# Input modulation one feature block further ahead, an earlier second weight block, and idle products between the first norm's steps

## The chip, the core and the metric

The kernel runs on one core of a Trainium2 chip. The core has a matrix engine (TensorE, PE in the rows), two engines for elementwise work (VectorE, DVE, and ScalarE, ACT), GpSimd (POOL) and a queue that issues transfers (SyncE, SP). Each works through its own list of instructions in order and waits for others by semaphores. The metric is the time of one execution on the device, in microseconds.

## What is computed

One layer of a hybrid transformer over 512 latent tokens and 256 context tokens, 1024 features wide. The part that matters here is its beginning: both streams are normalized and modulated, then projected. The context goes through the same weights with its own modulation vector.

```python
mod = jax.nn.silu(c) @ w_mod[layer] + b_mod[layer]
sh1, sc1, gt1, sh2, sc2, gt2 = jnp.split(mod[:, None, :], 6, axis=-1)
...
h = modulate(rmsnorm(x, g_norm_mix[layer]), sh1, sc1)          # h * (1 + scale) + shift
hc = modulate(rmsnorm(ctx, g_norm_mix[layer]), csh1, csc1)
mix_lat, mix_ctx = token_mixer(h, hc, cos, sin, layer, w_in[layer], ...)
```

Behind it come latent attention, a gated linear recurrence in both directions, an output projection, a second norm, a SwiGLU feed-forward part and a last norm.

## The kernel before

Features lie on the partitions, in 8 blocks of 128 (KT = 8); tokens lie along the free axis. Weights come in blocks of 128x1024 float32 (`make_unit`, L119 to L134): one transfer of 512 KB into a tile `wf` on SP's queue, a cast to `wh` on ScalarE (L132), the rest `wl` by subtraction on VectorE (L133). A main product is three matmuls, L150 to L152: high by high, high by low, low by high (`mm3`).

The first stage makes the modulated input and, at the same time, the first projection (`hi`, which fills `vt`). `squares` (L307, L309) adds up the squares of the 8 blocks of x in `acl`. After 32 matmuls on a tile of ones, which give nothing that is used (`warm`, L351, bank `pw`), `rstd_sums` (L174) sums `acl` over the partitions, `rstd_cols` works out 1/sqrt, `rstd_diag` (L207, L209) writes it on diagonals `rsd`, and `rstd_spread` (L216) spreads them to all partitions with four 128x128 matmuls.

The modulation of a feature block k has three steps. `modvec(k)` multiplies the block's columns of w_mod (two 512 KB transfers, `wms` or `wm`) by silu(c) in eight 32-column matmuls (L320) and copies the result from PSUM on VectorE (L323). `modsel(k)` picks the two vectors out of it with two small matmuls (L329) and makes scale and shift `ab` in three small VectorE operations (L332 to L334). `make_h(k)` then writes the block: L339 on VectorE (scale and norm), L340 on ScalarE (shift, cast to `hh`), L341 on VectorE (the rest, `hl`).

The loop at L376 goes over the blocks. In a round k stand the main products of block k for token tile 0, then `modsel(k + 1)` and `make_h(k + 1)`, the products of tile 1, `modvec(k + 2)`, and the products of tiles 2 and 3 (`g0_mm`). A weight block serves two feature blocks, so the second one is first needed at block 2, the third one at block 4. In between lie the squares of the context (from round 1), its sums (L174, round 2) and its spread (round 3); the context's products follow four rounds later. A scheduler with priorities makes the order of each engine from this code, so that neighbouring rounds overlap in it.

SP's queue is written out by hand in the line `for step in (...)`: a number up to 16 loads the columns `wm` up to there, two per feature block; 101 to 103 load the weight blocks 1 to 3; -1 and -2 load the halves of the context `xc`. Small SBUF tiles hold `modvec`'s result: `spk` for even blocks, `modsb` for odd ones.

Of the kernel before, what the change touches and what calls it, by code (L numbers as in the profile page):

```python
# [18 lines left out]
P = 128  # L19
DM = 1024  # L20
KT = DM // P
NL = 512
# [30 lines left out]
def block_kernel(ctx: ExitStack, tc: tile.TileContext, xT, ctxT, vec, cin, cst, msk, wm, wmt, wi, wqkv, wo, wgu, wd, out):  # L53
    nc = tc.nc
# [7 lines left out]
    def nm(s):  # L62
        uid[0] += 1
        return f"{s}_{uid[0]}"
# [4 lines left out]
    def sm():  # L69
        return psum.tile([P, 512], F32, tag="sm", name=nm("sm"), bufs=4)  # L70
# [15 lines left out]
    ones = L0.tile([P, P], F32, name="ones")  # L86
# [10 lines left out]
    def C(name):  # L97
        a, b = CC[name]
        return cs[:, a:b]
# [40 lines left out]
    def prefetch(n):  # L140
        while len(made) < min(n, len(units)):
            make_unit(len(made))
# [97 lines left out]
    for p, tag, n in ((E, "eb", 3), (E, "ea", 2), (D, "da", 2), (D, "db", 2), (D, "dc", 2)):  # L240
        t = p.tile([P, n, UNIT], F32, tag=tag, name=nm("wms"), bufs=1)
        wsp += [t[:, i, :] for i in range(n)]
    B = pool("B", "right")
    hh = B.tile([P, KT, NL], F32R, name="hh")
    hl = B.tile([P, KT, NL], F32R, name="hl")
# [3 lines left out]
    xs = A.tile([P, KT, NL], F32, name="xs")  # L249
# [14 lines left out]
            nc.sync.dma_start(f, wm[u])  # L264
            wms.append(f)

    for step in (2, 101, 4, 6, -1, 102, 8, -2, 10, 12, 103, 14, 16):
        if step < 0:
            nc.sync.dma_start(xc[:, -4 * step - 4 : -4 * step, :], ctxT[:, -4 * step - 4 : -4 * step, :])
        elif step > 100:  # L270
            prefetch(step - 100)
        else:
            load_wm(step)
# [38 lines left out]
    rl, rc = acl, acc  # L312

    def modvec(k):
        ps = sm()
        for j in range(2):
            f = wms[2 * k + j]
            for kk in range(4):
                g = kk
                nc.tensor.matmul(ps[32 * g : 32 * g + 32, :256], csil[:, 4 * j + kk, :], f[:, kk * 256 : (kk + 1) * 256],  # L320
                                 start=(j == 0), stop=(j == 1), skip_group_check=True, tile_position=(0, 32 * g))
        sb = A.tile([P, 256], F32, tag="modsb", name=nm("modsb"), bufs=1) if k % 2 else spk[:, NL:]
        nc.vector.tensor_copy(sb, ps[:, :256])  # L323
        return sb

    def modsel(k, sb):
        p2 = sm()
        for j in range(2):
            nc.tensor.matmul(p2[:, 2 * j : 2 * j + 2], sb[:, j * P : (j + 1) * P], C("sel"), start=True, stop=True,  # L329
                             skip_group_check=True)  # L330
        ab = A.tile([P, 4], F32, tag="ab", name=nm("ab"), bufs=KT)
        nc.vector.tensor_scalar(ab[:, 0:2], p2[:, 0:2], bm[:, 8 + k : 9 + k], 1.0, op0=ALU.add, op1=ALU.add)  # L332
        nc.vector.tensor_scalar(ab[:, 0:2], ab[:, 0:2], V("gmix")[:, k : k + 1], None, op0=ALU.mult)
        nc.vector.tensor_scalar(ab[:, 2:4], p2[:, 2:4], bm[:, k : k + 1], None, op0=ALU.add)  # L334
        return ab

    def make_h(src, r, n, k, ab, j, oh, ol):
        t = temp(n)
        nc.vector.scalar_tensor_tensor(t, src[:, k, :], ab[:, j : j + 1], r, op0=ALU.mult, op1=ALU.mult)  # L339
        nc.scalar.activation(oh[:, k, :], t, AF.Identity, bias=ab[:, 2 + j : 3 + j])  # L340
        nc.vector.scalar_tensor_tensor(ol[:, k, :], t, ab[:, 2 + j : 3 + j], oh[:, k, :].bitcast(F32), op0=ALU.add,  # L341
                                       op1=ALU.subtract)
# [4 lines left out]
    pw = sm()  # L347

    def warm(n):
        for _ in range(n):  # L350
            nc.tensor.matmul(pw[:, :P], ones, ones, start=True, stop=True, skip_group_check=True)  # L351

    warm(32)
    cols = rstd_cols(A, rstd_sums([acl], NL), DM, fast=True)
    sb = modvec(0)
    dg = rstd_diag(A, cols)
    abs_ = [modsel(0, sb)]
    pb = rstd_spread(dg)
    make_h(xs, pb, NL, 0, abs_[0], 0, hh, hl)
    nc.scalar.copy(rl, pb)  # L360
    sb = modvec(1)
    g0 = [big(), big()]
    vacc = [g0[0][:, 0, :], g0[0][:, 1, :], g0[1][:, 0, :], g0[1][:, 1, :]]

# [11 lines left out]
    for k in range(max(KT, lag + KT // 2)):  # L376
        if k < KT:
            g0_mm(k, (0,))
        if k + 1 < KT:
            abs_.append(modsel(k + 1, sb))  # L380
            make_h(xs, rl, NL, k + 1, abs_[k + 1], 0, hh, hl)
        if k == 1:
            squares(xc, acc, NC)
        if k == lag - 2:
            ccols = rstd_cols(A, rstd_sums([acc], NC), DM, fast=True)
        if k == lag - 1:
            rc = rstd_spread(rstd_diag(A, ccols))
            nc.scalar.copy(acc, rc[:, :NC])
            rc = acc
        if k < KT:  # L390
            g0_mm(k, (1,))
            if k + 2 < KT:
                sb = modvec(k + 2)
            g0_mm(k, (2, 3))
        if k >= lag - 1:
            for kc in range((k + 1 - lag) * 2, min(KT, (k + 2 - lag) * 2)):
                make_h(xc, rc, NC, kc, abs_[kc], 1, gh, gl)
        if k == lag:
            vacc += [sm(), sm()]
        if k >= lag:  # L400
            for kc in range((k - lag) * 2, min(KT, (k + 1 - lag) * 2)):
                g0_mm(kc, (4, 5))
# [41 lines left out]
    for j in range(2):  # L444
        t = HG.tile([P, 4, P], F32, name=f"am{j}")
# [447 lines left out]
    for i in range(len(seq)):  # L893
# [10 lines left out]
        h, t = seq[i]  # L904
# [258 lines left out]
```

## Time and profile before

| | |
|---|---|
| median of 3 runs | 794.73 us (791.47 to 798.05) |
| the profiled execution | 792.62 us, of it span 790.8 us |
| TensorE busy | 768.1 us, 97% of the span |
| VectorE, ScalarE busy | 446.9 us (57%), 311.4 us (39%) |
| TensorE's granted clock, mean over the span | 0.988 |
| transfers | 88.77 MB, mean 112 GB/s |

The span is the time from the first to the last instruction of the profiled execution; some 1.8 us lie around it. Times in the rows are counted from the span's start. A granted clock of 1.00 is 2.4 GHz, 0.50 is 1.2 GHz. In a row of the timeline the bracket at the end tells how long the engine was idle before it and what ended that. Matmuls are pipelined, so the distance between two starts tells more than a single duration; a product of 32-bit operands counts as two instructions there.

### The profile page before, as it was taken

The page shows a single profiled execution, that of the slowest core. Times are in us where ns is not written, and L with a number is a line of the kernel's source. Part 1 is how long each engine was busy: PE and PEld are TensorE (multiplying, and loading weights), DVE is VectorE, ACT ScalarE, POOL GpSimd, SP SyncE. Part 2 cuts the span into 40 slices and gives each one's busy share as a digit, 9 for nine tenths or more (in the row PEclk, how much of TensorE's full clock was granted, in tenths as well). Part 3 has the DMA queues.
Part 4 walks back from the last instruction along what each step waited for, and adds up shares of the span by engine and source line. Part 5 has one row for each costly group of instructions (what it writes and reads, how often), then busy time and mean ns, then how long its engine had stood idle before and what let it go on. Part 6 is the DMA issues. An engine that isn't in the chain of part 4 may idle for free.

```text
span 790.8 us, 10832 instructions
## 1 busy us (share of the span) xinstructions
PE 768.1 (97%) x4342; PEld 631.7 (80%) x4342; DVE 446.9 (57%) x820; ACT 311.4 (39%) x569; POOL 10.1 (1%) x18
## 2 busy tenths in 40 slices
PE   8899999999999989999999999999999999999995
PEld 7568878788887768888999888888888888888885
DVE  5576569839778989985566434432333233223324
ACT  6344246434544577664344223222322222212211
POOL 0000000000000100000000000000000000000000
PEclk8899999999999999999999999999999999999997
DMA  9923723311110022345403343423232323332303
GB/s 332 390 76 134 252 80 108 133 57 55 64 55 28 28 80 90 125 165 181 160 2 100 113 160 133 151 89 107 80 107 82 104 78 96 93 100 80 111 3 107
DMA packets 26706, 88.77 MB, mean 112 GB/s; under 512 B 2976, under 2 KB 5280, under 8 KB 26528
## 3 DMA queue, kind: packets, MB, share of 16 engines
q1 hardware_dynamic: 25568, 87.03, 33.0%
q10 hardware_dynamic: 1088, 1.05, 0.4%
q8 instruction: 34, 0.56, 0.3%
q14 instruction: 16, 0.13, 0.1%
HBM read 85.97 MB, written 2.10 MB: 111 GB/s over the span
## 4 chain that ended last, share of the span: by engine, by line
PE 89%; DVE 7%; ACT 2%; issue 1%; DMA 1%; SPq 0%; DVEq 0%; ACTq 0%
PE big L150 18%; PE big L151 17%; PE big L152 17%; PE sm L150 9%; PE sm L151 9%; PE sm L152 9%; PE big L857 2%; PE sm L604 1%; PE sm L876 1%; PE big L858 1%; PE sm L320 1%; DVE U L585 1%; PE sm L598 1%; DVE acl L309 1%; DVE G L506 1%
## 5 line engine op out<-in xcount | busy, mean ns | idle before, releaser
L133 DVE TENSOR_TENSOR wl<-wf,wh 128x1024 fp32r<-128x1024 f32 (+2 forms) x100 | 119.6, 1196 | 186.3 <-ACT wh L132 186.2
L132 ACT CAST wh<-wf 128x1024 fp32r<-128x1024 f32 (+2 forms) x100 | 102.9, 1029 | 280.3 <-PE big L151 167.6
L150 PE MATMUL big<-h2h,wh 128*128 128x512 f32 (+1 forms) x368 | 140.3, 381 | 0.0
L151 PE MATMUL big<-h2l,wh 128*128 128x512 f32 (+1 forms) x368 | 140.0, 381 | 0.0
L152 PE MATMUL big<-h2h,wl 128*128 128x512 f32 (+1 forms) x368 | 140.0, 381 | 0.0
L151 PEld LDWEIGHTS big<-h2l,wh 128*128 128x128 f32 x368 | 69.2, 188 | 14.6
L150 PEld LDWEIGHTS big<-h2h,wh 128*128 128x128 f32 x368 | 69.2, 188 | 14.4
L152 PEld LDWEIGHTS big<-h2h,wl 128*128 128x128 f32 x368 | 69.2, 188 | 14.4
L150 PE MATMUL sm<-ah,wh 128*128 128x512 f32 (+1 forms) x198 | 73.5, 371 | 0.0
L152 PE MATMUL sm<-ah,wl 128*128 128x512 f32 (+1 forms) x198 | 73.4, 371 | 0.0
L151 PE MATMUL sm<-al,wh 128*128 128x512 f32 (+1 forms) x198 | 73.4, 370 | 0.0
L427 DVE SCALAR_TENSOR_TENSOR wl<-wl,cs 128x1024 f32<-128x1024 f32 x32 | 39.0, 1220 | 33.8 <-DMA wl<-in_wmt_dram 33.8
L150 PE MATMUL big<-wh,hh 128*128 128x512 f32 x96 | 40.2, 422 | 3.3 <-ACT hh L340 1.9
L150 PEld LDWEIGHTS sm<-ah,wh 128*128 128x128 f32 x198 | 37.3, 188 | 7.1
L151 PEld LDWEIGHTS sm<-al,wh 128*128 128x128 f32 x198 | 37.3, 188 | 7.1
L152 PEld LDWEIGHTS sm<-ah,wl 128*128 128x128 f32 x198 | 37.3, 188 | 7.1
L150 PE MATMUL big<-hh,wh 128*128 128x512 f32 x104 | 42.8, 412 | 0.0
L151 PE MATMUL big<-hl,wh 128*128 128x512 f32 x104 | 40.9, 394 | 0.0
L152 PE MATMUL big<-hh,wl 128*128 128x512 f32 x104 | 40.8, 392 | 0.0
L151 PE MATMUL big<-wl,hh 128*128 128x512 f32 x96 | 38.8, 406 | 0.0
L152 PE MATMUL big<-wh,hl 128*128 128x512 f32 x96 | 38.4, 402 | 0.0
L506 DVE RECIPROCAL G<-S 128x528 f32<-128x528 f32 x8 | 27.5, 3432 | 0.1
(326 smaller groups left out, 1353.4 us busy)
## 6 DMA issues: line engine op xcount, KB each, us to landing
wf<-in_wgu_dram SPq DMA_DIRECT2D x44, 512.0 KB, 3.4
wl<-in_wmt_dram SPq DMA_DIRECT2D x32, 512.0 KB, 3.5
wf<-in_wi_dram SPq DMA_DIRECT2D x25, 512.0 KB, 3.9
wf<-in_wd_dram SPq DMA_DIRECT2D x16, 512.0 KB, 3.5
wms<-in_wm_dram SPq DMA_DIRECT2D x11, 512.0 KB, 9.6
wf<-in_wo_dram SPq DMA_DIRECT2D x8, 512.0 KB, 3.5
wf<-in_wd_dram SPq DMA_DIRECT2D x8, 384.0 KB, 3.1
wm<-in_wm_dram SPq DMA_DIRECT2D x5, 512.0 KB, 10.2
```

Source lines behind the costliest of these rows:

```text
L132: nc.scalar.copy(hi[:, :w], f[:, :w])
L133: nc.vector.tensor_sub(lo[:, :w], f[:, :w], hi[:, :w].bitcast(F32))
L150: nc.tensor.matmul(o, lh, rh, start=start, stop=False, skip_group_check=True)
L151: nc.tensor.matmul(o, lh, rl, start=False, stop=False, skip_group_check=True)
L152: nc.tensor.matmul(o, ll, rh, start=False, stop=stop, skip_group_check=True)
L309: nc.vector.tensor_add(acc_, acc_, sq_)
L320: nc.tensor.matmul(ps[32 * g : 32 * g + 32, :256], csil[:, 4 * j + kk, :], f[:, kk * 256 : (kk + 1) * 256], start=(j == 0), stop=(j == 1), ...
L427: nc.vector.scalar_tensor_tensor(f, f, 1.0, sc, op0=ALU.mult, op1=ALU.mult, accum_out=acc)
L506: nc.vector.reciprocal(I, S)
L585: nc.vector.scalar_tensor_tensor(U[:, c1, :], U[:, c0, :], er[:, 1, c0 : c0 + 1], U[:, c1, :], op0=ALU.mult, op1=ALU.add)
L598: nc.tensor.matmul(t, a2[:, j, :], vt[:, j, h * P : (h + 1) * P], start=True, stop=False, skip_group_check=True)
L857: nc.tensor.matmul(ps[:, 0, :], L, R[:, :NL], start=(i == 0), stop=(i == 4), skip_group_check=True)
```

## The change

Three things. The second weight block (102) is loaded as what follows the fourth pair of transfers in the list, ahead of the columns of block 2, where it stood behind those and the first half of the context. `modsel` and `make_h` run two blocks ahead of the products in a round and `modvec` three, where it was one and two; block 1 is made before the loop, with the norm read straight from PSUM (`pb`). And `warm_on` adds 3 idle products behind `modvec(0)`, on its copied result, and 8 behind `modvec(1)`, on the last diagonal; they write to `pw` and nothing reads it.

```diff
-    for step in (2, 101, 4, 6, -1, 102, 8, -2, 10, 12, 103, 14, 16):
+    for step in (2, 101, 4, 102, 6, 8, -1, 10, -2, 12, 103, 14, 16):
...
+    def warm_on(t, n):
+        for _ in range(n):
+            nc.tensor.matmul(pw[:, :P], ones, t, start=True, stop=True, skip_group_check=True)
+
     warm(32)
     cols = rstd_cols(A, rstd_sums([acl], NL), DM, fast=True)
-    sb = modvec(0)
+    sbs = [modvec(0)]
+    warm_on(sbs[0][:, :P], 3)
     dg = rstd_diag(A, cols)
-    abs_ = [modsel(0, sb)]
+    abs_ = [modsel(0, sbs[0])]
     pb = rstd_spread(dg)
     make_h(xs, pb, NL, 0, abs_[0], 0, hh, hl)
     nc.scalar.copy(rl, pb)
-    sb = modvec(1)
+    sbs.append(modvec(1))
+    warm_on(dg[0][:, 3, :], 8)
+    abs_.append(modsel(1, sbs[1]))
+    make_h(xs, pb, NL, 1, abs_[1], 0, hh, hl)
+    sbs.append(modvec(2))
...
-        if k + 1 < KT:
-            abs_.append(modsel(k + 1, sb))
-            make_h(xs, rl, NL, k + 1, abs_[k + 1], 0, hh, hl)
+        if k + 2 < KT:
+            abs_.append(modsel(k + 2, sbs[k + 2]))
+            make_h(xs, rl, NL, k + 2, abs_[k + 2], 0, hh, hl)
...
-            if k + 2 < KT:
-                sb = modvec(k + 2)
+            if k + 3 < KT:
+                sbs.append(modvec(k + 3))
```

What the scheduler makes of it is seen in the engines' lists. TensorE from `modvec(0)` to the first main products, before (`sm` are small PSUM tiles, `big` those of the main products, `wms` columns of w_mod):

```order
L320 MATMUL sm_241<-wms_77,csil 32x256 x8
L329 MATMUL sm_256<-cs,spk 128x2 x2
L216 MATMUL sm_263<-rsd_251,ones 128x128 x4
L320 MATMUL sm_273<-wms_77,csil 32x256 x4
L150 MATMUL big_284<-wh_110,hh 128x512
L150 MATMUL big_285<-wh_110,hh 128x512
L151 MATMUL big_284<-wl_111,hh 128x512
L151 MATMUL big_285<-wl_111,hh 128x512
L320 MATMUL sm_273<-wms_78,csil 32x256 x4
```

and the same place in the change (L355 are the idle products):

```order
L320 MATMUL sm_241<-wms_77,csil 32x256 x8
L355 MATMUL sm_194<-spk,ones 128x128 x3
L329 MATMUL sm_259<-cs,spk 128x2 x2
L216 MATMUL sm_266<-rsd_254,ones 128x128 x4
L355 MATMUL sm_194<-rsd_254,ones 128x128 x2
L320 MATMUL sm_276<-wms_77,csil 32x256 x4
L355 MATMUL sm_194<-rsd_254,ones 128x128 x5
L320 MATMUL sm_276<-wms_78,csil 32x256 x4
L355 MATMUL sm_194<-rsd_254,ones 128x128
L150 MATMUL big_315<-wh_110,hh 128x512
```

All of `modvec(1)` and all eleven idle products stand ahead of the first main product now; before, half of `modvec(1)` stood behind four of them.

TensorE around the sums of the context norm (L174), before; the rows that follow these up to the first product of block 4 are the selection, the spread and two `modvec` among six main products:

```order
L150 MATMUL big_284<-wh_121,hh 128x512
L151 MATMUL big_284<-wl_122,hh 128x512
L150 MATMUL big_285<-wh_121,hh 128x512
L151 MATMUL big_285<-wl_122,hh 128x512
L152 MATMUL big_284<-wh_121,hl 128x512
L174 MATMUL sm_387<-ones,acc 128x2 x2
L320 MATMUL sm_402<-wms_80,csil 32x256 x4
L320 MATMUL sm_402<-wms_81,csil 32x256 x4
```

and in the change, from the selection products of block 4 to the first product of block 4 with the third weight block (`wh_135`):

```order
L329 MATMUL sm_408<-cs,spk 128x2 x2
L152 MATMUL big_315<-wh_118,hl 128x512
L151 MATMUL big_316<-wl_119,hh 128x512
L152 MATMUL big_316<-wh_118,hl 128x512
L150 MATMUL big_316<-wh_118,hh 128x512
L151 MATMUL big_316<-wl_119,hh 128x512
L152 MATMUL big_316<-wh_118,hl 128x512
L174 MATMUL sm_418<-ones,acc 128x2 x2
L320 MATMUL sm_433<-wms_81,csil 32x256 x4
L320 MATMUL sm_433<-wm_131,csil 32x256 x4
L329 MATMUL sm_453<-cs,modsb_442 128x2 x2
L216 MATMUL sm_467<-rsd_464,ones 128x128 x2
```

The next row there is the product of block 4. The sums moved from the start of block 3's products to their end, and selection and spread follow them without a main product in between. VectorE has, in the change, between the selection of block 4 (`ab_411`) and the context norm's columns:

```order
L333 TENSOR_SCALAR ab_411<-ab_411,vc 128x2
L339 SCALAR_TENSOR_TENSOR spk<-xs,ab_411,acl 128x512
L309 TENSOR_TENSOR acc<-acc,sp_75 128x256 x2
L341 SCALAR_TENSOR_TENSOR hl<-spk,ab_411,hh 128x512
L309 TENSOR_TENSOR acc<-acc,sp_75 128x256 x2
L191 TENSOR_SCALAR rsv_421<-sm_418 128x2
```

The last of the additions to `acc`, which the sums read, now stand behind the modulation of block 4; before, they stood behind that of block 3. On ScalarE the cast of the second weight block (`wh_121` before, `wh_118` now) moved from behind the modulation of block 2 to ahead of that of block 1, and the cast of the third one from behind the first context blocks to right behind the context norm's diagonal. From the end of the loop on, the lists are the same but for a few neighbours that change places on SP and VectorE.

## Rows read from the trace of the kernel before

**Rows 1.** The page: TensorE's busy time; shares of the chain that ended last.

```profile
PE 768.1 (97%) x4342; PEld 631.7 (80%) x4342; DVE 446.9 (57%) x820; ACT 311.4 (39%) x569; POOL 10.1 (1%) x18
...
PE 89%; DVE 7%; ACT 2%; issue 1%; DMA 1%; SPq 0%; DVEq 0%; ACTq 0%
```

**Rows 2.** Stretches of time: length, engines' busy time (instructions), clock, DMA share, GB/s.

```profile
13.50:14.00 0.50, 0.50 (x15) 0.26 (x8) 0.28 (x3) 0.16 (x1) 0.00 (x0) 0.94 1.01 410
...
20.00:21.00 1.00, 1.00 (x3) 0.81 (x3) 0.68 (x2) 0.11 (x1) 0.00 (x0) 0.50 1.03 406
...
24.00:24.50 0.50, 0.50 (x5) 0.41 (x4) 0.00 (x0) 0.00 (x0) 0.00 (x0) 0.82 1.03 410
...
35.00:40.00 5.00, 3.71 (x24) 2.77 (x26) 3.39 (x10) 1.14 (x2) 0.00 (x0) 1.00 0.75 301
...
50.00:90.00 40.00, 40.00 (x200) 32.32 (x199) 27.16 (x46) 12.85 (x17) 1.94 (x6) 1.00 0.48 163
```

**Rows 3.** Timeline of TensorE: start, length, instruction, [idle before, what ended it].

```profile
12.30 1.05 PE L174 MATMUL sm<-ones,acl 128*128 128x2 f32 x8 [0.96 <-DVE acl L309]
...
15.17 1.01 PE L329 MATMUL sm<-cs,spk 128*128 128x2 f32 x4 [0.53 <-DVE spk L323]
16.04 2.06 PE L216 MATMUL sm<-rsd,ones 128*128 128x128 f32 x8
18.03 1.08 PE L320 MATMUL sm<-wms,csil 128*32 128x256 f32 x8
19.70 1.22 PE L150 MATMUL big<-wh,hh 128*128 128x512 f32 x2 [0.58 <-ACT hh L340]
...
24.54 0.71 PE L152 MATMUL big<-wh,hl 128*128 128x512 f32 x2
25.17 0.64 PE L320 MATMUL sm<-wms,csil 128*32 128x256 f32 x8
25.74 0.50 PE L150 MATMUL big<-wh,hh 128*128 128x512 f32 x1
26.08 0.40 PE L151 MATMUL big<-wl,hh 128*128 128x512 f32 x1
26.31 0.40 PE L152 MATMUL big<-wh,hl 128*128 128x512 f32 x1
...
31.79 0.50 PE L150 MATMUL big<-wh,hh 128*128 128x512 f32 x1 [1.08 <-ACT wh L132]
...
35.38 0.50 PE L329 MATMUL sm<-cs,modsb 128*128 128x2 f32 x4
...
38.20 0.50 PE L150 MATMUL big<-wh,hh 128*128 128x512 f32 x1 [1.29 <-ACT hh L340]
...
39.47 0.53 PE L174 MATMUL sm<-ones,acc 128*128 128x2 f32 x4
...
46.08 0.73 PE L150 MATMUL big<-wh,hh 128*128 128x512 f32 x2 [0.35 <-ACT wh L132]
```

**Rows 4.** Timeline of VectorE, as rows 3.

```profile
14.69 0.42 DVE L323 COPY spk<-sm 128x256 f32<-128x256 f32 x1 [0.16 <-PE sm L320]
...
18.80 1.22 DVE L133 TENSOR_TENSOR wl<-wf,wh 128x1024 fp32r<-128x1024 f32 x1
...
38.85 0.42 DVE L309 TENSOR_TENSOR acc<-acc,sp 128x256 f32<-128x256 f32 x1
```

**Rows 5.** Timeline of ScalarE, as rows 3.

```profile
26.70 0.40 ACT L307 ACTIVATE acc<-xc 128x256 f32<-128x256 f32 x1
...
30.08 0.72 ACT L340 ACTIVATE hh<-t,ab 128x512 fp32r<-128x512 f32 x1 [2.06 <-DVE t L339]
30.71 1.03 ACT L132 CAST wh<-wf 128x1024 fp32r<-128x1024 f32 x1
```

**Rows 6.** SP's issue of the second weight block; from issue to landing, us, last number.

```profile
11.74 0.33 SPq L122 DMA_DIRECT2D wf<-in_wi_dram  x1
...
wf<-in_wi_dram SPq DMA_DIRECT2D x1, 512.0 KB, 11.2
```

## The prediction

> **What bounds the kernel now.** I read the page's first part and its chain of waits, then stretches of time with clock and engine load, then the first 50 us of TensorE, VectorE and ScalarE instruction by instruction, then the transfers. TensorE is busy 97% of the span and carries 89% of the chain that ended last [rows 1]. From 50 to 90 us it is busy all of the 40 us [rows 2]. So what the edit wins or loses before 46 us arrives at the end; and from the end of the loop that the diff touches on, the order of work on every engine is the old one again, bar two or three neighbours that change places. What has to be found is one shift: when the first main product of feature block 4 (L150, 46.08 us [rows 3]) starts, and how fast TensorE runs just behind it.
>
> Up to that point TensorE loses time in two ways. It waits: 0.58 us before the first main product, 1.08 for the cast of the second weight block, 1.29 for a modulated block, 0.35 for the third weight block [rows 3]. And its clock is at the lower level (0.50, 1.2 GHz) from 13.94 us (a mean of 0.94 in the half microsecond from 13.5 is 0.44 at 1.00 and 0.06 at 0.50) to 24.18 (0.82 in that from 24.0) [rows 2]. What it did before that fall: 0.96 us idle, then 1.05 us of 128x2 products [rows 3] and some of the 32-column ones behind them. Before the rise it had run main products and 32-column ones without a pause since 19.70, 4.48 us.
>
> **The transfers.** The second weight block moves three places up in SP's queue; the pairs that it passes (modulation columns 2) come one place later, the context halves three and two. At 406 GB/s [rows 2] a place of 512 KB is 1.29 us. The block landed at 11.74 + 11.2 = 22.9 us and was cast only at 30.71 [rows 5, 6], so the transfer was not what was waited for: the cast stood behind the modulation of block 2 in ScalarE's order (30.08 [rows 5]). In the new order it stands before block 1, and that takes the 1.08 us away. For that move the transfer must be earlier too: it lands at 22.9 - 3.9 = 19.0, before the cast can start. The first context half, one place ahead of it, landed at 21.6; now it lands 3 x 1.29 later, at 25.5, and is first read at 26.70 before [rows 5], later now. Columns 4 and 5, one place later, are read after 25 us and land by 21. So the transfers cost nothing; if a context half were late, its squares would wait on ScalarE, and the sums of the context norm after them. The last places are the same ones, so the queue ends no later.
>
> **The idle products.** Eleven 128x128 products go into TensorE's own order, so what stands behind them waits. Four such products took 2.06 us at the lower clock (L216 [rows 3]), from start to next start (18.03 - 16.04) / 4 = 0.50 each, of which I take 0.48 for one that follows another, and half that at the upper one. Three stand before the selection products of block 0, which still wait for the same copy and so start at 15.17 + 3 x 0.48 = 16.6 instead of 15.17. They fill nothing: they wait for the copy too. The spread then ends at 18.03 + 1.45 = 19.5. Two more bring TensorE to 20.45, with 32-column products (1.08 [rows 3]), five idle ones, 32-column products again and one idle one to come before the first main product. That is 5.04 us at the lower clock and 2.6 at the upper one, since 32-column products take 0.57 there [rows 3]. The first main product starts at 25.5 or at 23.1; were the clock up from the spread on, 21.5. The modulated block needs 19.5 + 1.67 = 21.2, by the distance from the spread's end to the product that waited for it (18.03 to 19.70 [rows 3]). So the old wait of 0.58 us is covered, by a longer one in the queue. VectorE's subtraction of the first weight block (1.22 us [rows 4]) moves ahead of L339 into VectorE's wait for the spread, so it costs nothing, and would cost up to 1.22 if the spread ended early. I take 23.1: TensorE then has no pause from 15.17 on, where before it had one at 19.1. That is 3.4 us later than 19.70.
>
> **From the first main product to block 4.** Before: 46.08 - 19.70 = 26.38 us. Out go the waits of 1.08, 1.29 and 0.35, half of the 4.48 us at the lower clock (2.24) and the second half of a modulation product that is done earlier now (0.57). That leaves 20.85. There are three fewer changes from main to modulation products and back; by the spacing of 24.54 to 26.08 (two main products, one group, one main product: 1.54, against 3 x 0.23 + 0.57) [rows 3] a change costs 0.27, so 20.05.
>
> In come new waits. The sums for the context norm (L174) stood behind five main products of block 3 that had themselves waited 1.29 us; the last addition ended at 38.85 + 0.42 = 39.27 and L174 started at 39.47, with no wait [rows 3, 4]. Now only six main products (1.4 us) stand between the selection products of block 4 and L174, and VectorE still needs those products, then L339, two additions, L341 and two more. From the selection products to the last addition the old order took 39.27 - 35.38 = 3.9 us [rows 3, 4]; TensorE has 0.5 for the selection (35.38) and 6 x 0.23 of work. So a wait of about 2.0 us is new, and block 4 is queued behind it. Right behind it the next selection products wait for the copy of theirs (0.42, as the 14.69 one [rows 4]), and block 4 for the cast of the third weight block, which now stands behind the context norm's diagonal on ScalarE: its column arithmetic and a cast of 1.03 us (30.71 [rows 5]) leave about 0.3 us. Bounds of the three together: 1.2 if the additions run between other work, 3.6 if nothing overlaps. I take 2.0 + 0.45 + 0.3 = 2.75, and block 4 starts at 23.1 + 20.05 + 2.75 = 45.9, 0.2 earlier than 46.08. The two halves cancel.
>
> **The clock a second time.** Between the last main product of block 3 and the first of block 4 TensorE now has some 5.2 us with no main product: 2.0 idle, 128x2 sums, 32-column products, 0.45 idle, selection, spread, 0.3 idle. The fall at 13.94 followed just such a mixture, and less idle time (0.96 us). Against it: the idle 1.29 us before 38.20, between main products, left the clock at 1.00 (35 to 40 us) [rows 2, 3]. I take the fall as likelier, since the new stretch is nearest to the first row. Then selection and spread take twice their time (0.5 + 0.5 more, 0.3 of it under the cast), 0.7; and block 4 starts at half speed. For how long I take the 4.48 us before the rise at 24.18: 2.24 us lost. Sum: -0.2 + 0.7 + 2.2 = **+2.7 us**; bounds of this clock part 0 and 4.
>
> The Trainium skill, in "TensorE: Matmul & The Clock Gate", section "A second HAM failure mode: psum-queue depth-cycling", says that frequent short pauses between groups of products make the clock swing between its levels and that throughput is lost in the swings. The rows of 31.79 and 38.20 us do not agree for single pauses, the fall at 13.94 does for a group of them. By the rule the sum is +2.7, by those two rows -0.2.
>
> L339 of block 1 reads the spread from PSUM instead of its copy, as block 0 did before; I cost that at nothing, since it saves the wait for the copy.
>
> **Against the times shown.** The sum is made on 792.62 us (span 790.8) and gives 795.3. The median of the runs is 2.1 higher; 794.73 + 2.7 = **797.4**.
>
> **Rivals.**
> - *No second fall.* Waits as above, clock as at 38.20. The two halves cancel: 794.5. For it speaks the row of 35 to 40 us, against it the 128x2 and 32-column products that follow the wait.
> - *Not slower.* The filled queue brings the clock up as soon as the spread (first main product at 21.5), and it does not fall later: 1.6 us more off the first half, 792.9; if the additions get between other VectorE work and the new waits shrink to 1.2, 791.4. It decides from where the first main product starts before about 23.1 and the clock stays at 1.00 through the context sums. For it: TensorE is busy without a pause from 15.17. Against it: selection and 32-column products are small, and the same ones did not hold the clock before.
> - *The idle products run at the lower clock throughout.* First main product at 25.5, then everything as forecast: 794.73 + 2.7 + 2.4 = 799.8. For it: the rise at 24.18 came only after main products.
> - *The lead changes nothing.* The waits of 1.08 and 1.29 stay, as VectorE's chain per block is what it was. Then block 4 starts 2.4 later and the new waits shrink by as much: no other time than the forecast's, so it has no chance of its own.
>
> **How the numbers follow.** Forecast 0.50, with 795.5 to 798.5 as its own range (the clock part 1 to 4); no second fall 0.20; not slower 0.15; lower clock throughout 0.15. The three runs lie 3.3 us to either side of the median. The range 792.0 to 800.5 leaves out the lower part of "not slower" and the upper part of the last case, under 2 in 10. About 1%, 8 us, is what a measurement of this kernel can tell from no change: no case reaches 786.8 or 802.7. So 0.95 for within 1%, 0.02 faster, 0.03 slower for what I have not seen.
>
> **What would show it.** In the changed profile: the first main product at about 23.1 us (21.5 or 25.5 for rivals); no wait before block 1, 2 and 3; TensorE waiting about 2 us for L309 in front of L174; block 4 between 46 and 47; a granted clock of 0.50 somewhere from 44 to 52 us. If the last is missing the forecast is nearly 3 us too high; if the wait before L174 is missing, the whole middle part is wrong and the kernel is faster.

## The result, and the profile after

The changed kernel takes 796.5 us (median; 794.78 to 797.0) against 794.57 us (790.51 to 798.05) for the kernel before in the same comparison: a ratio of 1.0031, with a 95% interval of 1.0016 to 1.0046. That is a small loss, well inside the 1% that was called no change, and 0.9 us under the forecast of 797.4. The profiled execution took 795.11 us, 2.5 more than that of before.

The page of the changed kernel, busy times and the shares of the chain that ended last (as [rows 1]):

```profile
PE 769.5 (97%) x4364; PEld 633.8 (80%) x4364; DVE 447.4 (56%) x820; ACT 311.3 (39%) x569; POOL 10.1 (1%) x18
...
PE 89%; DVE 7%; ACT 2%; issue 1%; DMA 1%; SPq 0%; DVEq 0%; ACTq 0%
```

TensorE has 22 instructions more (eleven idle products count as two each) and is otherwise as before. So these totals tell nothing here; the first 50 us do. TensorE's timeline of the changed kernel (columns as in [rows 3]):

```profile
13.13 1.05 PE L174 MATMUL sm<-ones,acl 128*128 128x2 f32 x8 [2.38 <-DVE acl L309]
...
15.74 1.34 PE L355 MATMUL sm<-spk,ones 128*128 128x128 f32 x6 [0.56 <-DVE spk L323]
16.87 0.85 PE L329 MATMUL sm<-cs,spk 128*128 128x2 f32 x4
17.59 2.05 PE L216 MATMUL sm<-rsd,ones 128*128 128x128 f32 x8
...
20.02 0.64 PE L320 MATMUL sm<-wms,csil 128*32 128x256 f32 x8
...
22.71 0.48 PE L150 MATMUL big<-wh,hh 128*128 128x512 f32 x1
...
40.22 0.39 PE L152 MATMUL big<-wh,hl 128*128 128x512 f32 x1
42.97 0.58 PE L174 MATMUL sm<-ones,acc 128*128 128x2 f32 x4 [2.36 <-DVE acc L309]
...
45.95 1.01 PE L329 MATMUL sm<-cs,modsb 128*128 128x2 f32 x4 [0.55 <-DVE modsb L323]
46.83 1.20 PE L216 MATMUL sm<-rsd,ones 128*128 128x128 f32 x4
47.68 1.20 PE L150 MATMUL big<-wh,hh 128*128 128x512 f32 x2
...
104.13 0.44 PE L706 MATMUL sm<-cs,mx 128*128 128x128 f32 x2 [0.90 <-DVE mx L676]
```

The three waits of before in front of blocks 2, 3 and 4 (blocks are counted from 0; 1.08, 1.29, 0.35 us [rows 3]) are gone: from 22.71 to 40.61 no row has a bracket, and block 4 at 47.68 has none. In their place stands one wait of 2.36 us, for the last addition of the context's squares, and one of 0.55 behind it. The last row is the first product of the next stage; the same product of the kernel before (its L697) starts at 101.10 us. The difference of 3.03 us stays nearly as it is to the last norm (784.11 against 781.12 us for its last sums). At the very end the clock falls later than in the execution before (the last spread takes 0.68 us against 1.19), which gives 0.5 back.

Stretches of the changed kernel (columns as in [rows 2]):

```profile
14.00:24.00 10.00, 9.44 (x76) 7.52 (x75) 4.99 (x15) 4.03 (x7) 0.00 (x0) 0.83 1.02 408
24.00:43.00 19.00, 16.62 (x108) 10.22 (x107) 12.54 (x31) 5.34 (x12) 0.00 (x0) 1.00 0.84 333
43.00:54.00 11.00, 10.46 (x67) 5.99 (x68) 7.55 (x23) 3.78 (x8) 0.00 (x0) 0.69 0.29 95
```

The granted clock falls twice. A mean of 0.83 over 10 us is 3.4 us at 0.50, where before had all of that stretch at 0.50; a mean of 0.69 over 11 us is 6.8 us at 0.50, where before had none.

VectorE's rows in front of the sums (L339 is the modulation of block 4, the last row holds the last two additions, which end at 42.82 us):

```profile
39.66 0.75 DVE L339 SCALAR_TENSOR_TENSOR spk<-xs,ab,acl 128x512 f32<-128x512 f32 x1
...
41.87 0.95 DVE L309 TENSOR_TENSOR acc<-acc,sp 128x256 f32<-128x256 f32 x2
```

Why the additions are late stands on ScalarE and in the transfers. ScalarE's timeline of the changed kernel (L340 writes `hh`, one row for each block; L307 are the context's squares):

```profile
25.63 0.72 ACT L340 ACTIVATE hh<-spk,ab 128x512 fp32r<-128x512 f32 x1 [3.03 <-DVE spk L339]
31.05 0.72 ACT L340 ACTIVATE hh<-t,ab 128x512 fp32r<-128x512 f32 x1 [4.70 <-DVE t L339]
31.68 0.40 ACT L307 ACTIVATE acc<-xc 128x256 f32<-128x256 f32 x1
31.99 1.01 ACT L307 ACTIVATE sp<-xc 128x256 f32<-128x256 f32 x3
35.56 0.72 ACT L340 ACTIVATE hh<-t,ab 128x512 fp32r<-128x512 f32 x1 [2.55 <-DVE t L339]
36.19 1.02 ACT L307 ACTIVATE sp<-xc 128x256 f32<-128x256 f32 x3
40.45 0.72 ACT L340 ACTIVATE hh<-spk,ab 128x512 fp32r<-128x512 f32 x1 [3.25 <-DVE spk L339]
41.08 0.40 ACT L307 ACTIVATE sp<-xc 128x256 f32<-128x256 f32 x1
```

The two context transfers of the changed kernel (first and last issue, and time to landing):

```profile
L269 SPq DMA_DIRECT2D xc<-in_ctxT_dram x2: 328/356/383, 15.0 to 18.9; - x2
...
DMA to landing us min/median/max: 10.9/11.0/11.0
```

The first half of the context is there at 15.0 + 11.0 = 26.0 us. ScalarE is done with the row of 25.63 (block 1) at 26.35 and has nothing to do until 31.05. The squares could run in that gap. They do not, because in ScalarE's list they stand behind the activation of block 2, which is not ready. Before, they stood ahead of it, behind that of block 1, and ran at 26.70 [rows 5]. This is the reading from which the second half of the experiments starts.

One thing that the section on the change doesn't name belongs to it: the new list of transfers moves more than the weight block. Each half of the context also goes behind one more pair of columns (8 stands ahead of -1 now, 10 ahead of -2). So "the moved transfer" below stands for both moves, until the last four runs separate them.

### The profile page after: what moved, and what is told of

Read it like the earlier page. It is cut to its first block, busy times and chain, and to the rows that moved or that the text cites. A ratio compares the mean times of both kernels' runs of the same rounds, so it can differ in the third digit from the quotient of the medians.

```text
span 793.3 us, 10876 instructions
## 1 busy us (share of the span) xinstructions
PE 769.5 (97%) x4364; PEld 633.8 (80%) x4364; DVE 447.4 (56%) x820; ACT 311.3 (39%) x569; POOL 10.1 (1%) x18
## 4 chain that ended last, share of the span: by engine, by line
PE 89%; DVE 7%; ACT 2%; issue 1%; DMA 1%; SPq 0%; DVEq 0%; ACTq 0%
PE big L150 17%; PE big L152 17%; PE big L151 17%; PE sm L150 9%; PE sm L151 9%; PE sm L152 9%; PE big L866 2%; PE sm L613 1%; PE sm L320 1%; PE sm L885 1%; PE big L867 1%; DVE U L594 1%; PE sm L607 1%; DMA xs<-in_xT_dram 1%; PE sm L216 1%
## 5 line engine op out<-in xcount | busy, mean ns | idle before, releaser
L133 DVE TENSOR_TENSOR wl<-wf,wh 128x1024 fp32r<-128x1024 f32 (+2 forms) x100 | 119.6, 1196 | 187.9 <-ACT wh L132 187.8
```

The lines of the kernel that those rows point to most:

```text
L133: nc.vector.tensor_sub(lo[:, :w], f[:, :w], hi[:, :w].bitcast(F32))
```

## The experiments

All were timed against the kernel before on their chip. The diffs are against the changed kernel unless another is named.

**The idle products.** The first four runs shared a chip, on which the kernel before took 792.99 us.

```diff
-    warm_on(sbs[0][:, :P], 3)
...
-    warm_on(dg[0][:, 3, :], 8)
```

> The change without its eleven idle products: lead and earlier weight block alone. Theory of three payments (idle products in the queue, a new wait in front of L174, a second fall of the clock): the first main product starts near 19.7 us again, the clock is low until about 24, TensorE still waits some 2.4 us for L309 in front of L174 and the clock still falls there, so the time stays above before by 1 to 2.5 us, ratio 1.001 to 1.003. Rival, the idle products are the whole loss: 1.5 to 2 us faster than before, ratio 0.998.

Measured: 797.58 us, 1.0059 (1.0040 to 1.0079), above the 1.001 to 1.003 that was expected. Without the idle products the change is not faster, so they are not its loss. By the two ratios (1.0059 against 1.0031) they earn some 2 us in it, but the two were measured in different comparisons and their intervals touch. Its stretches:

```profile
14.00:24.00 10.00, 8.87 (x54) 5.44 (x54) 4.76 (x15) 4.03 (x7) 0.00 (x0) 0.57 1.02 408
24.00:43.00 19.00, 18.98 (x108) 11.55 (x107) 10.64 (x28) 4.43 (x11) 0.00 (x0) 0.87 0.83 329
43.00:54.00 11.00, 8.11 (x50) 4.42 (x50) 7.37 (x21) 4.41 (x9) 0.00 (x0) 0.69 0.13 27
```

The first main product comes earlier (20.57 us), but the clock is low far into the main products (0.87 from 24 to 43 us), and the second fall is there too. The converse adds the idle products to the kernel before and nothing else:

```diff
 (against the kernel before)
...
+    warm_on(sb[:, :P], 3)
...
+    warm_on(dg[0][:, 3, :], 8)
```

> The kernel before with the eleven idle products alone, at the same places. Theory: the first main product starts at 22 to 23.5 us, the stretch at 0.50 behind it is gone, the waits of 1.08 and 1.29 us stay, no wait in front of L174 and no second fall; +0.5 us, between -0.5 and +1.5, ratio 0.999 to 1.002. Rival, the idle products are the whole loss: +2 to +3 us, ratio 1.003.

Measured: 793.43 us, 1.0000 (0.9979 to 1.0020). By themselves they neither cost nor bring anything that can be measured. In its profile the first main product starts at 20.69 us, earlier than expected, and of the wait of 1.08 us only 0.30 is left.

**The place of the sums.** The sums of the context norm one step later in the code, behind the next products, and its spread behind those of the round:

```diff
-        if k == lag - 2:
-            ccols = rstd_cols(A, rstd_sums([acc], NC), DM, fast=True)
-        if k == lag - 1:
-            rc = rstd_spread(rstd_diag(A, ccols))
...
+            if k == lag - 1:
+                ccols = rstd_cols(A, rstd_sums([acc], NC), DM, fast=True)
             g0_mm(k, (2, 3))
+        if k == lag - 1:
+            rc = rstd_spread(rstd_diag(A, ccols))
```

> The change with the sums of the context norm (L174) one round later and their spread behind that round's products, so that block 4 no longer stands behind them; nothing else is moved in the code. Theory: no wait over 0.6 us and no second fall before 55 us; block 4 starts 3.5 to 4.5 us earlier, and with the clock the kernel is 4 to 5 us faster than the change, 2 us faster than before, ratio 0.996 to 0.998. Rival, the idle products are the whole loss: as the change, 1.003.

Measured: 795.92 us, 1.0035 (1.0014 to 1.0056). The expectation fell. The wait of L174 is gone from TensorE, but two others took its place:

```profile
42.85 0.61 PE L329 MATMUL sm<-cs,modsb 128*128 128x2 f32 x4 [1.60 <-DVE modsb L323]
...
45.96 0.51 PE L151 MATMUL big<-wl,hh 128*128 128x512 f32 x1 [0.81 <-DVE wl L133]
```

The copy and the subtraction that these wait for stand on VectorE behind the same late additions. Moving the one who waits does not help if the work that is late stays late. The clock fell a second time here too, against the expectation:

```profile
43.00:54.00 11.00, 10.19 (x64) 5.89 (x65) 7.66 (x23) 3.21 (x8) 0.00 (x0) 0.84 0.27 95
```

**The second fall of the clock.** Ten idle products ahead of the sums, so that TensorE has no pause there:

```diff
         if k == lag - 2:
+            warm_on(sbs[k + 2][:, :P], 10)
             ccols = rstd_cols(A, rstd_sums([acc], NC), DM, fast=True)
```

> The change with ten more idle products behind the selection products of block 4, where TensorE would wait for L309. They take about 2.4 us at the upper clock, as long as the wait. Theory: the wait in front of L174 shrinks below 0.5 us, L174 itself starts at the same time, but the clock does not fall there (or falls later and for less), worth 1.4 to 2.1 us against the change: ratio to before 1.000 to 1.001. If the clock was not what the wait cost: as the change, 1.003.

Measured: 795.6 us, 1.0032 (1.0014 to 1.0051). The clock keeps its level and the time does not come back. Its stretch and its rows around the sums:

```profile
43.00:54.00 11.00, 9.65 (x80) 5.38 (x78) 8.71 (x26) 4.81 (x9) 0.00 (x0) 1.00 0.30 97
```

```profile
39.77 2.48 PE L355 MATMUL sm<-spk,ones 128*128 128x128 f32 x20
...
45.84 0.61 PE L329 MATMUL sm<-cs,modsb 128*128 128x2 f32 x4 [0.55 <-DVE modsb L323]
...
48.94 0.50 PE L151 MATMUL big<-wl,hh 128*128 128x512 f32 x1 [0.78 <-DVE wl L133]
```

The fill takes the place of the pause, 2.48 us for 2.36, and the row of 48.94 waits where the changed kernel had no wait. From the first main product to the product on `mx` this execution needs 79.51 us (23.54 to 103.05), 1.9 less than the changed kernel's 81.42. The medians don't show that gain (1.0032 against 1.0031, in different comparisons); which of the two is nearer to the worth of the second fall stays open.

**The parts one by one.** Up to here I held the lead for the cause. The next four runs share a chip (before: 793.41 us). The transfer alone, and the transfer put back:

```diff
 (against the kernel before)
-    for step in (2, 101, 4, 6, -1, 102, 8, -2, 10, 12, 103, 14, 16):
+    for step in (2, 101, 4, 102, 6, 8, -1, 10, -2, 12, 103, 14, 16):
```

> The kernel before with one part of the change: the second weight block is asked for as the fourth pair of transfers. Theory A (the loss comes from the lead of one block, which puts the seven additions of the context's squares, the copy in front of the selection and the cast of the third weight block behind one another on VectorE): the transfer is innocent, 0.999 to 1.001 of the time before, with the wait for the second weight block's cast (1.08 us) still there or turned into another of the same size. Theory B (the modulation blocks that now come after the weight block land late and cost TensorE a wait): 1.002 to 1.004, with a wait of 1 to 3 us for a transfer on line 320.

```diff
-    for step in (2, 101, 4, 102, 6, 8, -1, 10, -2, 12, 103, 14, 16):
+    for step in (2, 101, 4, 6, -1, 102, 8, -2, 10, 12, 103, 14, 16):
```

> The changed kernel with the second weight block's transfer put back to its old place; lead and idle products stay. Theory A (the loss comes from the lead): 1.002 to 1.004 of the time before, as the changed kernel itself (1.003), with the wait of line 174 for the additions (2.4 us) still there. Theory B (the loss comes from the moved transfer): 0.999 to 1.001. In case the lead needs the weight block early, a wait of 0.5 to 2 us for the second weight block stands in front of feature block 2's products and the time is 1.004 to 1.006.

Measured: the transfer alone 792.62 us, 0.9985 (0.9965 to 1.0005); the change without it 793.43 us, 0.9999 (0.9978 to 1.0019). The first agrees with theory A, the second speaks against it: lead and idle products together lose nothing as long as the transfer stays where it was. TensorE around the sums in the change without the moved transfer:

```profile
40.79 0.59 PE L174 MATMUL sm<-ones,acc 128*128 128x2 f32 x4
...
44.57 0.61 PE L329 MATMUL sm<-cs,modsb 128*128 128x2 f32 x4 [0.83 <-DVE modsb L323]
...
47.68 0.50 PE L151 MATMUL big<-wl,hh 128*128 128x512 f32 x1 [0.91 <-DVE wl L133]
```

L174 has no wait, and main products of block 3 stand behind it. The squares are back behind block 1's activation on ScalarE (27.01 us).

The additions on GpSimd, in the order of the change:

```diff
-                nc.vector.tensor_add(acc_, acc_, sq_)
+                (nc.gpsimd if n == NC else nc.vector).tensor_add(acc_, acc_, sq_)
```

> The changed kernel with the seven additions of the context's squares on GpSimd in place of VectorE; all else as in the change. Theory A (VectorE's load between feature blocks 2 and 4 is what the lead makes late): the wait of 2.4 us at line 174 is gone or under 1 us, and the copy in front of block 4's selection comes earlier; if that is all of it, 1.000 to 1.001 of the time before. Theory C (the order of TensorE's own work, with nothing behind block 3 to fill a pause, makes the loss whoever does the additions): 1.002 to 1.004, and another wait of 1 to 2 us between blocks 3 and 5. GpSimd's time for one such addition is not in the trace before; if it is over 1.5 us, the wait of line 174 stays, and the run tells only GpSimd's price.

Measured: 793.62 us, 1.0000 (0.9980 to 1.0021), and the loss is gone. The row of GpSimd, and TensorE's behind the sums:

```profile
35.78 3.36 POOL L309 TENSOR_TENSOR acc<-acc,sp 128x256 f32<-128x256 f32 x4 [2.02 <-ACT sp L307]
```

```profile
39.49 0.50 PE L174 MATMUL sm<-ones,acc 128*128 128x2 f32 x4
...
42.94 0.61 PE L329 MATMUL sm<-cs,modsb 128*128 128x2 f32 x4 [1.95 <-DVE modsb L323]
```

The squares still stand behind block 2's activation (30.62 us), but GpSimd ends its last addition at 39.14 us, where VectorE in the change ended it at 42.82 (a pair from 41.87, 0.95 long, behind block 4's modulation). L174 waits for nothing. Another wait of 1.95 us remains, as theory C had it, but not its price, and the clock from 43 to 54 us is 1.00.

The change without the lead:

```diff
 (against the kernel before)
-    for step in (2, 101, 4, 6, -1, 102, 8, -2, 10, 12, 103, 14, 16):
+    for step in (2, 101, 4, 102, 6, 8, -1, 10, -2, 12, 103, 14, 16):
...
+    warm_on(sb[:, :P], 3)
...
+    warm_on(dg[0][:, 3, :], 8)
```

> The change without the lead: the kernel before with the idle products and the moved transfer. Theory A (the lead makes the loss): 0.998 to 1.001 of the time before, no wait of line 174, and feature block 4 starts about 31 us behind the first sums, as with the idle products alone. Theory B (the moved transfer makes it): 1.002 to 1.004.

Measured: 792.51 us, 0.9997 (0.9978 to 1.0016). So the lead is needed for the loss, and the moved transfer too. Neither makes it with the idle products alone. That left theory A wrong, and the idle gap on ScalarE as what the two do together.

**The order of the squares.** The last four runs share a chip (before: 794.21 us); the first of them is the changed kernel once more, as a control.

> The changed kernel itself once more, on the chip of the other runs of this call, as the control: 1.002 to 1.005 of the time before, with the wait of 2.4 us at line 174 and a second fall of TensorE's clock near 43 to 46 us. If it stands within 1.001 of before here, the runs that undid one part and came out at 1.000 tell nothing.

Measured: 796.36 us, 1.0023 (1.0003 to 1.0042). The loss is there again. Its profiled execution took 798.21 us; stretches and TensorE's rows:

```profile
14.00:24.00 10.00, 9.45 (x57) 7.05 (x58) 4.66 (x14) 3.67 (x7) 0.00 (x0) 0.54 1.03 409
24.00:43.00 19.00, 18.98 (x128) 12.04 (x126) 10.78 (x28) 4.68 (x11) 0.00 (x0) 1.00 0.81 323
43.00:54.00 11.00, 8.09 (x50) 4.35 (x50) 7.42 (x21) 4.53 (x9) 0.00 (x0) 0.69 0.16 42
```

```profile
22.18 1.08 PE L320 MATMUL sm<-wms,csil 128*32 128x256 f32 x8
...
25.32 0.48 PE L150 MATMUL big<-wh,hh 128*128 128x512 f32 x1
...
45.55 0.58 PE L174 MATMUL sm<-ones,acc 128*128 128x2 f32 x4 [2.37 <-DVE acc L309]
```

The order and the waits are those of the first profile; the first stretch at the lower clock is longer, and the first main product, the sums and the product on `mx` come 2.6 us later (25.32, 45.55, 106.70). The gap on ScalarE is there too, and clearer: the context's first half landed at 14.8 + 10.5 = 25.3 us, ScalarE had nothing to do from 28.97 to 33.65, and the squares ran at 34.28. Then the change with each half of the context asked for one step earlier, the weight block still fourth (this expectation and the next count the blocks from 1; by the count from 0 they mean the activations of blocks 1 and 2):

```diff
-    for step in (2, 101, 4, 102, 6, 8, -1, 10, -2, 12, 103, 14, 16):
+    for step in (2, 101, 4, 102, 6, -1, 8, -2, 10, 12, 103, 14, 16):
```

> The changed kernel with the context's first transfer asked for one step earlier, ahead of modulation blocks 6 and 7 (steps 2, 101, 4, 102, 6, -1, 8, ...); the weight block stays the fourth pair. On ScalarE's order the first four squares of the context then stand behind block 2's activation and ahead of block 3's; in the change they stand behind block 3's. Theory D (the loss is that with the moved transfer the squares stand one block later in ScalarE's order, and the lead has left nothing for TensorE to do when their sum is late): the squares start near 26 to 27 us in place of 31.7, the wait of line 174 is under 0.5 us, and the time is 0.998 to 1.001. Theory A (the lead by itself): 1.002 to 1.004 as the change.

Measured: 793.66 us, 1.0000 (0.9986 to 1.0014), 2.7 us under the control by the medians. ScalarE and TensorE:

```profile
26.88 0.73 ACT L340 ACTIVATE hh<-spk,ab 128x512 fp32r<-128x512 f32 x1 [3.11 <-DVE spk L339]
27.51 0.40 ACT L307 ACTIVATE acc<-xc 128x256 f32<-128x256 f32 x1
```

```profile
41.80 0.59 PE L174 MATMUL sm<-ones,acc 128*128 128x2 f32 x4
...
45.59 0.61 PE L329 MATMUL sm<-cs,modsb 128*128 128x2 f32 x4 [0.83 <-DVE modsb L323]
...
48.69 0.50 PE L151 MATMUL big<-wl,hh 128*128 128x512 f32 x1 [0.91 <-DVE wl L133]
```

The squares start right behind the activation of 26.88 (block 1), the wait of L174 is gone, and the clock from 43 to 54 us is 1.00. The converse leaves the weight block almost where it was, fifth instead of sixth, and puts the context two steps later:

```diff
-    for step in (2, 101, 4, 102, 6, 8, -1, 10, -2, 12, 103, 14, 16):
+    for step in (2, 101, 4, 6, 102, 8, -1, 10, -2, 12, 103, 14, 16):
```

> The converse: lead and idle products, the second weight block only the fifth pair (behind modulation blocks 4 and 5), and the context's first transfer two steps later than before. The squares stand behind block 3's activation on ScalarE, as in the change. Theory D: the squares start at 31 to 32 us, the wait of 2 to 2.5 us at line 174 is back, and the time is 1.002 to 1.004 though the weight block's place is nearly that of before. Otherwise (it is the weight block's place): 0.999 to 1.001.

Measured: 798.57 us, 1.0051 (1.0031 to 1.0072), and the wait is back:

```profile
46.35 0.58 PE L174 MATMUL sm<-ones,acc 128*128 128x2 f32 x4 [2.83 <-DVE acc L309]
```

The squares start at 33.04 us, behind the activation of 32.41 (block 2). All three numbers lie above what was expected (31 to 32 us, 2 to 2.5 us, 1.002 to 1.004), in the direction of theory D; this time is the median of 6 runs, those of most others of 12. Last, the lead alone:

```diff
-    for step in (2, 101, 4, 102, 6, 8, -1, 10, -2, 12, 103, 14, 16):
+    for step in (2, 101, 4, 6, -1, 102, 8, -2, 10, 12, 103, 14, 16):
...
-    warm_on(sbs[0][:, :P], 3)
...
-    warm_on(dg[0][:, 3, :], 8)
```

> Of the three parts the lead alone: no idle products, no transfer moved. Theory D: no wait of 2 us at line 174, 0.999 to 1.002 of the time before, since the squares keep their place behind block 2's activation; if the clock stays low longer without the idle products, as in the change without them (1.006), up to 1.003. Theory A (the lead by itself makes the loss): 1.003 to 1.006.

Measured: 794.89 us, 1.0009 (0.9987 to 1.0031), no wait at L174. The lead alone is no loss.

Together (the time from the first main product to the product on `mx` is that of one profiled execution each; in the row of before and in that of lead and transfer without idle products the clock was still low behind the first main product, and in the four with the wait it fell a second time):

| lead | transfer | idle | ratio (95%) | from first main product to `mx`, us | wait of L174, us |
|---|---|---|---|---|---|
| - | - | - | 1 | 81.40 | none |
| - | - | yes | 1.0000 (0.9979 to 1.0020) | 77.96 | none |
| - | yes | - | 0.9985 (0.9965 to 1.0005) | 78.67 | none |
| - | yes | yes | 0.9997 (0.9978 to 1.0016) | 77.36 | none |
| yes | - | - | 1.0009 (0.9987 to 1.0031) | 80.36 | none |
| yes | - | yes | 0.9999 (0.9978 to 1.0019) | 78.32 | none |
| yes | yes | - | 1.0059 (1.0040 to 1.0079) | 86.02 | 2.35 |
| yes | yes | yes | 1.0031 (1.0016 to 1.0046) | 81.42 | 2.36 |
| yes | yes | yes, again | 1.0023 (1.0003 to 1.0042) | 81.38 | 2.37 |
| yes | context earlier | yes | 1.0000 (0.9986 to 1.0014) | 78.83 | none |
| yes | context later | yes | 1.0051 (1.0031 to 1.0072) | 81.62 | 2.83 |

In this table the ratio is above 1 by more than its interval in just the four rows with the wait at L174. (Not in it are the run with the additions on GpSimd, 1.0000, and the two in which that wait was moved or filled; those stayed at 1.003, with the additions as late as in the change.) No version is faster than before by more than its interval; the nearest is the transfer alone.

## Why the prediction came out, and where it was wrong

**The sum was right, by terms that erred in both directions.** The forecast was +2.7 us by the profiles; they differ by 2.5, the medians by 1.9. Block 4 starts 1.6 us later than before (47.68 against 46.08), where 0.5 was forecast (-0.2 + 0.7); from there to `mx` another 1.4 is lost, where 2.2 was forecast. That 2.5 is so near to 2.7 is in part luck: 0.8 of it lies ahead of the change, 0.5 was given back at the very end, and the second profile of the same kernel took 3.1 us more than the first.

**The first main product.** Forecast 23.1 us, rivals 21.5 and 25.5. Measured 22.71 in the first profile and 25.32 in the control. Both are the same queue of idle products. The clock is what differs. In the first profile the 32-column products of 20.02 already run at the upper clock (0.64 us); in the control the same ones, at 22.18, are still at the lower one (1.08). So the rival "lower clock throughout" was no rival but another execution of the same kernel, and one number for this place was too much. The argument for that rival, that the clock rose only after main products, did not hold: in both profiles it rose with none of them run. Of the 3.0 us by which the first profile is later there, 0.8 is not the change's: L174 already stood at 13.13 instead of 12.30, waiting for the additions of x.

**The waits in front of blocks 2 and 3** (the forecast's 1.08 and 1.29 us). Forecast gone, and gone.

**The new waits.** Forecast 2.0 + 0.45 + 0.3, measured 2.36 + 0.55 + 0. The place, the sign and the size were right, since the order of the engines was read row by row. The third term did not show up: the cast of the third weight block is done at 46.07 us, before it is needed. Where the clock stayed up behind the sums, another wait stands at that place: 0.78 to 0.91 us for VectorE's subtraction of that block (L133; the runs with the fill, without the moved transfer and with the context earlier). The forecast had no term for it; in the changed kernel, whose products run at the lower clock there, no such wait shows.

**The run of products between them.** Forecast 20.05 without waits. Measured from 22.71 to 47.68 are 24.97 us; less 2.91 of waits and about 1.9 lost at the lower clock, from 43.42 us on (a mean clock of 0.92 from 43.0 to 43.5 is 0.08 us at 0.50; half of 47.68 - 43.42 - 0.55), that is 20.2.

**The second fall of the clock.** Forecast to cost 0.7 + 2.2 = 2.9 us. Measured: 6.8 us at 0.50, 0.5 of it idle, so half of 6.3 = 3.1. It is also visible in single rows: the selection at 45.95 takes 1.01 us here and 0.61 in the run with the context earlier, the spread 1.20 against 0.69. What went before it was a pause of 2.36 us and, behind small products, one of 0.55; in the run with the sums one step later it was pauses of 1.60 and 0.81 us, and there the clock fell too. In the run with the additions on GpSimd pauses of 1.95 and 0.91 us left it at 1.00. So the length of the pauses does not tell these cases apart, and what does stays open. In "TensorE: Matmul & The Clock Gate" of the Trainium skill, section "A second HAM failure mode: psum-queue depth-cycling", frequent short pauses between groups of products make the clock swing. The pauses here are two, not many: the changed kernel and the run with the later sums agree with it as far as that goes, the run on GpSimd does not.

**What was wrong is the cause of the new wait.** The prediction read the wait itself rightly: six main products against VectorE's chain from the selection of block 4 to the last addition. What it got wrong is what in the edit puts the additions there. It said "So the transfers cost nothing". It had even the condition in hand ("if a context half were late, its squares would wait on ScalarE, and the sums of the context norm after them"), and took it for settled because the context half would land in time. It did land in time, at 26.0 us for a gap on ScalarE that opened at 26.35. The failed step is that landing in time is enough. ScalarE's list is fixed ahead, and its order turned with the order of the transfers in the code: with the context two steps later the first four squares stand behind the activation of the next block, and so the additions one block later on VectorE. With the context one step earlier than in the change, the first four squares stand where they stood before, and the loss is gone; with it two steps later and the weight block only fifth, the loss is there. Why the scheduler turns the order was not seen, only that it turns with the list; what is shown is that the order, not the data, held the squares back.

**Why it takes the lead too.** With the transfer alone the squares also stand a block later (29.67 us), and nothing is lost. VectorE and TensorE of that run:

```profile
34.73 2.01 DVE L309 TENSOR_TENSOR acc<-acc,sp 128x256 f32<-128x256 f32 x4
```

```profile
36.98 0.50 PE L174 MATMUL sm<-ones,acc 128*128 128x2 f32 x4
```

The additions end at 36.74, and L174 starts at 36.98 behind products of block 3, which had themselves waited 0.59 us for `hh`; block 4's modulation (L339) comes only at 40.19. The lead takes that wait away and brings block 4's modulation forward. With the lead alone the last additions still come ahead of it, and they end at 38.24 us, ahead of L174 at 39.82. With both, they stand behind it: L339 of 39.66 waits for the selection products of block 4, TensorE has run out of block 3's products at 40.61, and a sum that ends at 42.82 is what it stands and waits for. The rival "the lead changes nothing" did not occur, since the waits of 1.08 and 1.29 us are gone.

**The idle products.** Costed as a delay of the first main product, they are one (20.57 without them, 22.71 and 25.32 with them). What the sum lacked is what the change would cost without them: 1.0059 instead of 1.0031, the clock staying low into the main products. Where TensorE has no wait at L174 they are worth nothing that can be measured (1.0000; 0.9999 against 1.0009; 0.9997 against 0.9985).

## What to carry to other kernels

When an edit moves a transfer, look in the engines' lists at where the operations that read the moved data now stand, and not only at whether the data still land in time: an operation that has its data can stand behind one that has not. A stage made ready earlier shows the next latest thing, so two edits that each cost nothing can cost together; test them one by one and in pairs. If a wait moves along when the one who waits is moved, the work in front of it is what is late.

## What the runs showed of the hardware

The length of the first stretch at the lower clock differs between executions of one kernel by more than this change is worth: from 14 to 24 us the mean granted clock was 0.83 and 0.54 in two profiles of the changed kernel, 0.50 in the kernel before, and with the idle products in the kernel before 1.00 (0.66 in three other kernels that have them). Two profiles of the same kernel lay 3.1 us apart (795.11 and 798.21), so a difference of 2 us between two single profiles of this kernel tells nothing; the medians and the presence of a wait do.

Four additions of 128x256 on GpSimd took 3.36 us, 0.84 each, where two on VectorE took 0.95, 0.48 each. The slower engine gave the earlier sum, since nothing else stood in its list there.
